# Retention branch's products in sevens, one sum of each block kept in PSUM, and the output weights' low halves on VectorE, in a two-layer gated trunk

## The chip, the cores and the metric

The kernel runs on one core of a Trainium2 chip. The metric is the device time of one execution in microseconds (us); the time of a version is the median of several runs. Engines are named as in the profile: PE (TensorE matmul), PEld (TensorE's weight loads), DVE (VectorE), ACT (ScalarE), POOL (GpSimd), SP (the engine that here only issues DMAs).

## The reference, cut to what matters

Two layers run over 640 tokens (512 noisy ones and 128 of context) with 1024 channels. Each layer makes three branches of 512 channels (retention, latent attention, Fourier mixing). What the change touches is the end of a layer, where each branch is projected to 1024 channels, weighed by a sigmoid gate that is itself a product of the layer's input `h`, summed, and projected once more:

```
branches = jnp.stack([o_r * jax.nn.silu(rz), o_m * jax.nn.silu(mz), o_f * jax.nn.silu(fz)], axis=2)
proj = jnp.einsum('btnw,nwd->btnd', branches, w_branch)
merged = jnp.sum(proj * jax.nn.sigmoid(gl.reshape(B, T, N_BRANCH, D_MODEL)), axis=2)
x = x + gate * (merged @ w_out)
```

All is float32. The kernel gets that precision from a faster matmul type by splitting each operand into a high and a low half and adding three products (high by high, high by low, low by high).

## The kernel before

**The merge stage.** For each of two layers the stage goes through three branches, in the loop over `n`: attention (`n` = 0), retention (`n` = 1), Fourier (`n` = 2). For each branch it goes over four blocks of 256 output channels (the loop over `i`). A block has two parts. The gates' part multiplies `h` (1024 channels) by a piece of `w_in` and ends in a tanh; the products' part multiplies the branch (512 channels) by a piece of `w_branch`, and its result is combined with the gates and added to `mg`, the merged sum. Tokens go in two halves of 320, output channels in two halves of 128.

**Sevens.** `seven` computes a 2 by 2 block product with seven products in place of eight (Winograd's form of Strassen's scheme: sums of the operands are made first, by `hidden_sums`, `branch_sums` and `wsums`). Each product adds into a PSUM bank of 320 columns. Three banks serve one call: A collects products 0, 1, 3 and 5 and is read after each of them, B holds product 2, C products 4 and 6. ACT copies A to SBUF after products 0, 1 and 3, and DVE adds B or C to such a copy. Products 5 and 6 are left to `rest`, which the next call of `seven` pours out by `flush` after its own product 0. A product of the gates' part has 12 matmuls, one of the products' part 6.

**Four.** For the retention branch alone (`n` = 1) the products' part is done by `four`: plain products, 4 accumulations of 12 matmuls, with weights split by `br_plain` and the branch split by `branch_split`. DVE then multiplies each accumulation by the gate straight from PSUM (L1086) and adds to `mg` (L1092).

**PSUM.** There are 8 banks. In this stage `bank` has 6 buffers, and `fill` and `po` take one each (small products for the next modulation vectors run between the others, L187 and L196).

**The output projection.** After the last block, `merge` (L81 on ACT, L82 on DVE) splits `mg` into high and low halves, one row of 128 channels after the other. The weights `w_out` come in 8 tiles of 128x1024: SP loads a tile into one of two `raw` buffers, ACT casts the high half, and the low half is a subtraction (`low`, L74) by DVE for the first tile and by POOL for the other seven. A `raw` buffer is free again when the low half has been made.

**Order.** The order of instructions on each engine is not the order of the code: a scheduler places each where its inputs are ready by its own estimate. Each engine then works through its list in order, and an instruction that waits holds up those behind it.

Of the kernel before, what the change touches and what calls it, by code (L numbers as in the profile page):

```python
# [8 lines left out]
F32 = mybir.dt.float32  # L9
# [5 lines left out]
P = 128  # L15
# [15 lines left out]
def build(nc, tc, A, O):  # L31
# [26 lines left out]
    def bank():  # L58
        return psum["p"].tile([P, 512], F32, name="bank", tag="bank", bufs=6)[:, :320]
# [47 lines left out]
    def rows(w, k0, nk, c0, n):  # L107
        return w[k0 * P:(k0 + nk) * P, c0:c0 + n].rearrange("(k p) n -> p k n", p=P)
# [953 lines left out]
    def br_plain(l, idx, c0):  # L1062
        r = wraw(rows(A["w_branch"][l, idx], 0, 4, c0, 256), 4, 256)
        w = wtiles(4, 256)
        split(w[0], w[1], r, leng=DVE)
        return w

    def branch_split(gp, src):
        for w in range(4):
            hi, lo = (gp.tile([P, 2, 320], F32R, name=f"bq{2 * w + i}", tag=f"bq{2 * w + i}", bufs=1) for i in range(2))  # L1070
            split(hi, lo, h2(src[:, w, :]))
            yield hi, lo

    def four(ws, xs, y2, ms, ps, tick, mid=None, fin=None):
        for j in range(2):
            for h, hs in enumerate(HALF):
                A = bank()
                for k in range(4):
                    for i, (u, v) in enumerate(PASSES):
                        PE.matmul(A, ws[u][:, k, j * P:(j + 1) * P], xs[k][v][:, h, :], start=(k == 0 and i == 0),  # L1080
                                  stop=(k == 3 and i == 2))
                if not (j or h):
                    flush()
                    if mid:
                        mid()
                DVE.scalar_tensor_tensor(ps[j][:, hs], y2[j][:, hs], 1.0, A, op0=ALU.add, op1=ALU.mult)  # L1086
                tick(3 * h)
                if fin:
                    DVE.tensor_tensor(ms[j][:, hs], ms[j][:, hs], ps[j][:, hs], op=ALU.add)
                    fin(j, hs)  # L1090
            if not fin:
                DVE.tensor_tensor(ms[j], ms[j], ps[j], op=ALU.add)  # L1092

# [6 lines left out]
    def seven(ws, xs, y1, y2, last, done, tick):  # L1100
# [16 lines left out]
        ACT.copy(y1[:, a], A)  # L1117
        tick(0)
        flush()
        B = bank()  # L1120
        product(B, 2, True)
        add(y1[:, a], y1[:, a], B)
# [64 lines left out]
    for l in range(DEPTH):  # L1187
# [26 lines left out]
        with ExitStack() as s:  # L1214
# [3 lines left out]
            fillp(), pout()  # L1218
            blocks = [(0, b) for b in range(8, 12)] + [(1, b) for b in range(8)] if l == 0 else [(1, b) for b in range(8, 12)]
# [12 lines left out]
            seven(w0, hq, *zs, lambda ps: ACT.copy(zs[0][:, b], ps), fourier_done, lambda i: None)  # L1232
# [6 lines left out]
            def gates(y2, n, bq, parts, np_):  # L1239
                def last(ps):  # L1240
                    ACT.activation(y2[0][:, b], ps, AF.Tanh, scale=0.5)

                def fin(j):
                    y = y2[j][:, a] if j == 0 else y2[j]
                    ACT.activation(y, y, AF.Tanh, scale=0.5)
# [8 lines left out]
                return last, fin, tick  # L1254

            def products(y2, n, ms, ps):
# [3 lines left out]
                def fin(j):  # L1260
                    y, m, p = y2[j], ms[j], ps[j]
                    s_ = a if j == 0 else slice(0, TT)
                    DVE.scalar_tensor_tensor(p[:, s_], y[:, s_], 1.0, p[:, s_], op0=ALU.add, op1=ALU.mult)
                    if n:
                        DVE.tensor_tensor(m, m, p, op=ALU.add)
                def tick(i):
                    if i in (3, 6):
                        next(steps, None)

                return last, fin, tick  # L1270

            for n, (idx, src, tmp) in enumerate(((1, omt, None), (0, ort, om), (2, ort, om))):
                if n:
                    flush()
                parts = branch_split(gp, src) if n == 1 else branch_sums(gp, src, bql)
                np_ = 4 if n == 1 else 7
# [183 lines left out]
```

## Time and profile before

| | |
|---|---|
| median of 3 runs | 1473.63 us (1472.76 to 1474.07) |
| the profiled execution's own time | 1475.04 us |
| its span, first to last instruction | 1473.3 us |
| PE busy | 1411.6 us, 96% of the span |
| DVE busy | 1025.5 us, 70% |
| ACT busy | 756.2 us, 51% |
| POOL busy | 239.1 us, 16% |
| merge stage, layer 1 / layer 2 | about 428 to 701 us / 1149 to 1401 us |

Busy time is the time in which at least one instruction of the engine ran. Matmuls overlap in their records, so a matmul's own duration (0.31 us for 320 columns) is longer than the distance to the next one, and the distance is what it costs. An engine that is not busy all the time still can hold others up, because of its order.

### The profile page before, as it was taken

What the parts mean: (1) busy time and instruction counts of PE and PEld (TensorE: products, weight loads), DVE (VectorE), ACT (ScalarE), POOL (GpSimd) and SP (SyncE); (2) the same over time, 40 slices, a digit from 0 to 9 for tenths busy, and PEclk for the clock granted to TensorE, in tenths of its full rate; (3) what the DMA queues carried; (4) which work ended last, traced back from release to release, by engine and by line L of the source; (5) the groups of instructions that cost most, each with busy time, mean ns of one, the idle gap of its engine ahead of it and who ended that gap; (6) DMA issues with size and microseconds to landing.
All of it is one profiled execution on the core that took longest, in us unless ns stands there. A gap on an engine that the chain in (4) does not pass through costs nothing.

```text
span 1473.3 us, 25184 instructions
## 1 busy us (share of the span) xinstructions
PE 1411.6 (96%) x9793; PEld 1345.2 (91%) x9793; DVE 1025.5 (70%) x1896; ACT 756.2 (51%) x1607; POOL 239.1 (16%) x227
## 2 busy tenths in 40 slices
PE   6999999999999999999999999999999999999997
PEld 4989989988988989999999899899889899999997
DVE  5367776666887686698573777765759778779843
ACT  5546666544545453455354566664545445445542
POOL 1220000301102211122312100021110112112240
PEclk9999999999999999999999999999999999999999
DMA  9520003331325474233532100042222433323342
GB/s 317 179 76 1 15 16 98 102 84 33 94 90 176 130 221 129 57 85 92 166 101 84 33 15 16 15 138 77 73 73 65 146 108 104 94 80 86 90 125 87
DMA packets 175847, 138.91 MB, mean 94 GB/s; under 512 B 8304, under 2 KB 168688, under 8 KB 175728
## 3 DMA queue, kind: packets, MB, share of 16 engines
q1 hardware_dynamic: 157680, 120.16, 28.1%
q10 hardware_dynamic: 18048, 17.15, 3.7%
q8 instruction: 77, 1.26, 0.4%
q14 instruction: 42, 0.34, 0.1%
HBM read 125.98 MB, written 11.30 MB: 93 GB/s over the span
## 4 chain that ended last, share of the span: by engine, by line
PE 74%; DVE 12%; DMA 5%; ACT 4%; issue 4%; POOL 1%; SPq 0%; POOLq 0%; ACTq 0%; DVEq 0%
PE bank L1109 25%; PE sm L85 6%; PE sm L87 5%; PE sm L86 5%; PE big L269 4%; PE bank L1080 4%; PE big L513 4%; PE fill L319 3%; PE sm L319 3%; PE sm L534 2%; PE sm L526 2%; DVE wl L74 2%; PE fill L187 2%; DMA raw<-in_w_in 1%; PE big L411 1%
## 5 line engine op out<-in xcount | busy, mean ns | idle before, releaser
L74 DVE TENSOR_TENSOR wl<-raw,wh 128x1024 fp32r<-128x1024 f32 (+5 forms) x146 | 153.8, 1055 | 87.3 <-ACT wh L78 39.0
L78 ACT CAST wh<-raw 128x1024 fp32r<-128x1024 f32 (+5 forms) x126 | 104.7, 833 | 86.2 <-DMA raw<-in_w_in 27.9
L1109 PE MATMUL bank<-hh,wh 128*128 128x320 f32 x416 | 130.0, 315 | 5.5 <-ACT tg L1125 4.4
L85 PE MATMUL sm<-wh,hh 128*128 128x256 f32 (+2 forms) x456 | 134.2, 295 | 0.5 <-DVE vl L74 0.5
L86 PE MATMUL sm<-wl,hh 128*128 128x256 f32 (+2 forms) x456 | 133.8, 294 | 0.0
L87 PE MATMUL sm<-wh,hl 128*128 128x256 f32 (+2 forms) x456 | 132.6, 294 | 0.0
L1109 PE MATMUL bank<-hl,wh 128*128 128x320 f32 x416 | 128.6, 310 | 0.0
L1109 PE MATMUL bank<-hh,wl 128*128 128x320 f32 x416 | 127.1, 311 | 0.0
L74 POOL TENSOR_TENSOR wl<-raw,wh 128x1024 fp32r<-128x1024 f32 (+1 forms) x32 | 66.4, 2075 | 294.9 <-ACT wh L78 215.7
L74 POOL TENSOR_TENSOR wl<-st,wh 128x512 fp32r<-128x512 f32 x26 | 38.0, 1463 | 328.8 <-ACT wh L78 328.8
L85 PEld LDWEIGHTS sm<-wh,hh 128*128 128x128 f32 x456 | 87.8, 193 | 2.2 <-issue 0.8
L1109 PEld LDWEIGHTS bank<-hh,wh 128*128 128x128 f32 x416 | 78.3, 188 | 11.9 <-ACT tg L1125 5.2
L86 PEld LDWEIGHTS sm<-wl,hh 128*128 128x128 f32 x456 | 87.8, 193 | 0.1
L87 PEld LDWEIGHTS sm<-wh,hl 128*128 128x128 f32 x456 | 87.4, 192 | 0.4 <-issue 0.4
L1109 PEld LDWEIGHTS bank<-hl,wh 128*128 128x128 f32 x416 | 78.5, 189 | 0.0
L1109 PEld LDWEIGHTS bank<-hh,wl 128*128 128x128 f32 x416 | 78.0, 189 | 0.0
L74 DVE TENSOR_TENSOR ptl<-sm,pth 128x384 fp32r<-128x384 f32 x128 | 67.2, 549 | 13.9 <-ACT pth L78 12.9
L1109 PE MATMUL bank<-bq,wh 128*128 128x320 f32 x320 | 72.0, 311 | 0.0
L78 ACT CAST pth<-sm 128x384 fp32r<-128x384 f32 x128 | 57.2, 481 | 22.6 <-PE sm L526 21.8
L78 ACT CAST wh<-st 128x512 fp32r<-128x512 f32 x68 | 39.6, 618 | 55.1 <-PE bank L1109 53.7
L640 DVE TENSOR_REDUCE nm<-big 128x1 f32<-128x768 f32 x64 | 60.7, 948 | 1.7 <-PE big L513 1.6
L74 DVE TENSOR_TENSOR wl<-st,wh 128x512 fp32r<-128x512 f32 x42 | 40.8, 972 | 29.5 <-ACT wh L78 27.0
(578 smaller groups left out, 4540.3 us busy)
## 6 DMA issues: line engine op xcount, KB each, us to landing
raw<-in_w_in SPq DMA_DIRECT2D x96, 512.0 KB, 4.0
mraw<-in_w_mod ACTq DMA_DIRECT2D x32, 512.0 KB, 4.0
raw<-in_w_branch SPq DMA_DIRECT2D x24, 512.0 KB, 3.6
mraw<-in_w_mod SPq DMA_DIRECT2D x16, 512.0 KB, 9.2
raw<-in_w_out SPq DMA_DIRECT2D x16, 512.0 KB, 4.3
raw<-in_w_in SPq DMA_DIRECT2D x8, 384.0 KB, 6.1
om<-xd SPq DMA_DIRECT2D x16, 192.0 KB, 3.5
xd<-xt SPq DMA_DIRECT2D x8, 320.0 KB, 4.2
```

The source lines that it names most:

```text
L74: eng.tensor_tensor(lo, src, hi.bitcast(F32), op=ALU.subtract)
L78: ACT.copy(hi, src)
L85: PE.matmul(out, ah, bh, start=first, stop=False)
L86: PE.matmul(out, ah, bl, start=False, stop=False)
L87: return PE.matmul(out, al, bh, start=False, stop=last)
L187: PE.matmul(ps[c:c + 32, :n], cs[:, 2 * (j + i):2 * (j + i) + 32], rv[:, i, :], start=(j + i < 4), stop=(j + i >= 4), tile_position=(0, c))
L269: PE.matmul(ps[:, 512 * h:512 * h + 320], ws[a][:, k, :], xs[b][k][:, 320 * h:320 * h + 320], start=(first and k == 0 and i == 0), stop=(l ...
L319: PE.matmul(ps, w[a][:, k, :], (hh, hl)[b][k][:, hs], start=(k == 0 and i == 0), stop=(k == NK - 1 and i == 2))
L513: PE.matmul(S[:, 512 * h:512 * h + 384], qT[hd][a][:, t * P:(t + 1) * P], (kth, ktl)[b][hd % 3][:, 384 * h:384 * h + 384], start=(i == 0), ...
L640: DVE.tensor_reduce(nm, Sv, axis=AX.XY if len(Sv.shape) == 3 else AX.X, op=ALU.max, negate=True)
L1080: PE.matmul(A, ws[u][:, k, j * P:(j + 1) * P], xs[k][v][:, h, :], start=(k == 0 and i == 0), stop=(k == 3 and i == 2))
L1109: PE.matmul(ps, w[u], x[v], start=(first and k == 0 and j == 0), stop=(k == n - 1 and j == 2), skip_group_check=True)
```

## The change

Three edits. First, the retention branch's products go through `seven` too; `four`, `br_plain` and `branch_split` are gone. Second, product 2 no longer has a bank of its own that DVE adds to a copy in SBUF: ACT copies A, after product 0, into a PSUM buffer of a new kind, `pair`, product 2 adds into that, and a new callback `begin` takes the sum from there (a tanh, a copy, or the multiplication by the gate). The first two pair buffers of a stage get one matmul beforehand (`marked`). `bank` falls from 6 buffers to 4, `pair` has 2. Third, the low halves of all eight `w_out` tiles are made by DVE.

```
-        return psum["p"].tile([P, 512], F32, name="bank", tag="bank", bufs=6)[:, :320]
+        return psum["p"].tile([P, 512], F32, name="bank", tag="bank", bufs=4)[:, :320]
+
+    marked = []
+
+    def pair():
+        return psum["p"].tile([P, 512], F32, name="pair", tag="pair", bufs=2)[:, :320]
...
-    def seven(ws, xs, y1, y2, last, done, tick):
+    def seven(ws, xs, y2, begin, last, done, tick):
...
         A = bank()
         product(A, 0, True)
-        ACT.copy(y1[:, a], A)
+        B = pair()
+        if len(marked) < 2:
+            marked.append(PE.matmul(B, ws[0][0][:, 0, :], xs[0][0][0], start=True, stop=True))
+        ACT.copy(B, A)
         tick(0)
         flush()
-        B = bank()
-        product(B, 2, True)
-        add(y1[:, a], y1[:, a], B)
+        product(B, 2, False)
+        begin(B)
         tick(1)
...
+                def begin(ps):
+                    ACT.activation(y2[0][:, a], ps, AF.Tanh, scale=0.5)
+
                 def fin(j):
-                    y = y2[j][:, a] if j == 0 else y2[j]
-                    ACT.activation(y, y, AF.Tanh, scale=0.5)
+                    if j:
+                        ACT.activation(y2[j], y2[j], AF.Tanh, scale=0.5)
...
                 def fin(j):
                     y, m, p = y2[j], ms[j], ps[j]
-                    s_ = a if j == 0 else slice(0, TT)
-                    DVE.scalar_tensor_tensor(p[:, s_], y[:, s_], 1.0, p[:, s_], op0=ALU.add, op1=ALU.mult)
+                    if j:
+                        DVE.scalar_tensor_tensor(p, y, 1.0, p, op0=ALU.add, op1=ALU.mult)
                     if n:
                         DVE.tensor_tensor(m, m, p, op=ALU.add)
+
+                def begin(acc):
+                    DVE.scalar_tensor_tensor(ps[0][:, a], y2[0][:, a], 1.0, acc, op0=ALU.add, op1=ALU.mult)
...
-                parts = branch_split(gp, src) if n == 1 else branch_sums(gp, src, bql)
-                np_ = 4 if n == 1 else 7
+                parts = branch_sums(gp, src, bql)
+                np_ = 7
...
-                    if n == 1:
-                        ends = (lambda: merge(4, 6), lambda j, hs: merge(6 + j, 7 + j, hs)) if (n, i) == (2, 3) else ()
-                        four(br_plain(l, idx, 256 * i), bq, y2, ms, ps, lambda i: next(steps, None) if i else None, *ends)
-                    else:
-                        seven(br_weights(wgp, l, idx, 256 * i), bq, *ps, *products(y2, n, ms, ps))
+                    seven(br_weights(wgp, l, idx, 256 * i), bq, ps[1], *products(y2, n, ms, ps))
...
-                eng = DVE if d == 0 else POOL
                 if d < 4:
-                    ws.append(wload(view, NK, P, eng))
+                    ws.append(wload(view, NK, P, DVE))
                 else:
                     rv = wraw(view, NK, P)
                     w = tuple(xp.tile([P, NK, P], F32R, name=n, tag=n, bufs=4) for n in ("xwh", "xwl"))
-                    split(*w, rv, leng=eng)
+                    split(*w, rv, leng=DVE)
```

How the order moves is shown at two places. The first is PE's list in layer 1, at the start of the gates' part of the retention branch's last block. Before (A is `bank_6905`, B `bank_6919`, C `bank_6946`):

```order
L1109 MATMUL bank_6905<-hh3_152,wl_6882 128x320
L1109 MATMUL bank_6919<-hh4_153,wh_6881 128x320
...
L1109 MATMUL bank_6919<-hh7_156,wl_6882 128x320
L1109 MATMUL bank_6946<-hq1h_4355,wh_6901 128x320
...
L1109 MATMUL bank_6946<-hq1h_4355,wl_6902 128x320
```

After (A is `bank_6921`, the pair buffer `pair_6934`; `bank_6826` belongs to the block before):

```order
L1082 MATMUL bank_6921<-hh3_152,wl_6898 128x320
L1082 MATMUL bank_6826<-bq8_6217,wh_6811 128x320
...
L1082 MATMUL bank_6826<-bq8_6217,wl_6812 128x320
L1082 MATMUL pair_6934<-hh4_153,wh_6897 128x320
L1082 MATMUL pair_6934<-hl4_161,wh_6897 128x320
...
L1082 MATMUL pair_6934<-hh7_156,wl_6898 128x320
```

Before, product 2 stood right behind product 0, into a bank that nothing else had touched; now six matmuls of the block before stand between them, and product 2 needs ACT's copy of A.

The second place is DVE's list at the end of layer 1's merge stage, from the last reads of the banks to the split of the last two rows. Before:

```order
L1113 TENSOR_TENSOR tg_7675<-bank_7763,tg_7675 128x320
L1258 SCALAR_TENSOR_TENSOR om_165<-tg_7674,bank_7817 128x320
L1265 TENSOR_TENSOR mg6_5129<-mg6_5129,om_165 128x640
L1113 TENSOR_TENSOR om_165<-bank_7868,om_165 128x320
L1263 SCALAR_TENSOR_TENSOR om_165<-tg_7675,om_165 128x640
L82 SCALAR_TENSOR_TENSOR hl6_163<-mg6_5129,hh6_155 128x640
L1265 TENSOR_TENSOR mg7_5130<-mg7_5130,om_165 128x640
L82 SCALAR_TENSOR_TENSOR hl7_164<-mg7_5130,hh7_156 128x640
```

After (`wl_7970` and `wl_7976` are the low halves of the third and fourth `w_out` tile):

```order
L1086 TENSOR_TENSOR tg_7712<-bank_7799,tg_7712 128x320
L79 TENSOR_TENSOR wl_7970<-raw_7967,wh_7969 128x1024
L1237 SCALAR_TENSOR_TENSOR om_165<-tg_7711,bank_7853 128x320
L1086 TENSOR_TENSOR om_165<-bank_7903,om_165 128x320
L1244 TENSOR_TENSOR mg6_5129<-mg6_5129,om_165 128x640
L1242 SCALAR_TENSOR_TENSOR om_165<-tg_7712,om_165 128x640
L79 TENSOR_TENSOR wl_7976<-raw_7973,wh_7975 128x1024
L1244 TENSOR_TENSOR mg7_5130<-mg7_5130,om_165 128x640
L87 SCALAR_TENSOR_TENSOR hl6_163<-mg6_5129,hh6_155 128x640
L87 SCALAR_TENSOR_TENSOR hl7_164<-mg7_5130,hh7_156 128x640
```

Two subtractions of 1024 columns, POOL's before, now stand in DVE's list among the steps that lead to `hl6` and `hl7`.

## Rows read from the trace of the kernel before

**Rows 1.** The page: PE's busy time, and the chain that ended last, by engine.
```profile
PE 1411.6 (96%) x9793; PEld 1345.2 (91%) x9793; DVE 1025.5 (70%) x1896; ACT 756.2 (51%) x1607; POOL 239.1 (16%) x227
...
PE 74%; DVE 12%; DMA 5%; ACT 4%; issue 4%; POOL 1%; SPq 0%; POOLq 0%; ACTq 0%; DVEq 0%
```
**Rows 2.** Stretches, layer 1's merge stage: length, busy us of PE, PEld, DVE, ACT, POOL.
```profile
465.00:545.00 80.00, 80.00 (x582) 72.98 (x582) 59.76 (x95) 40.15 (x77) 16.13 (x11) 1.00 0.57 168
545.00:625.00 80.00, 80.00 (x562) 75.80 (x562) 53.28 (x78) 32.23 (x55) 11.02 (x8) 1.00 0.34 95
625.00:690.00 65.00, 65.00 (x445) 65.00 (x444) 58.67 (x93) 34.02 (x66) 15.95 (x11) 1.00 0.32 89
```
**Rows 3.** PE's timeline in layer 1's retention branch: start, duration.
```profile
545.34 0.30 PE L1109 MATMUL bank<-hh,wh 128*128 128x320 f32 x1
...
547.10 0.46 PE L1080 MATMUL bank<-bq,wh 128*128 128x320 f32 x2
```
**Rows 4.** What wrote the banks from `four`: count, ns min/median/max.
```profile
L1080 PE MATMUL bank<-bq,wh x256: 305/309/413, 544.8 to 1322.8; 128*128 128x320 f32 x128
...
L1080 PE MATMUL bank<-bq,wl x128: 307/309/415, 545.2 to 1323.0; 128*128 128x320 f32 x128
```
**Rows 5.** DVE's adds of a bank to a copy (L1113), and their waits.
```profile
L1113 DVE TENSOR_TENSOR tg<-bank,tg x54: 472/481/492, 438.0 to 1399.8; 128x320 f32<-128x320 f32 x54
...
  PE bank L1109: 8.8, 12
```
**Rows 6.** Timeline: product 0's last matmul, and ACT's copy of its bank.
```profile
1389.85 0.31 PE L1109 MATMUL bank<-bq,wl 128*128 128x320 f32 x1
...
1390.20 0.43 ACT L1117 COPY om<-bank 128x320 f32<-128x320 f32 x1 [1.04 <-PE bank L1109]
```
**Rows 7.** Timeline: a copy that came late, and the matmul behind it.
```profile
688.54 0.31 PE L1109 MATMUL bank<-hh,wl 128*128 128x320 f32 x1
...
689.47 1.04 ACT L78 CAST wh<-raw 128x1024 fp32r<-128x1024 f32 x1
...
690.41 0.41 ACT L1131 COPY tg<-bank 128x320 f32<-128x320 f32 x1
...
690.87 0.41 PE L1109 MATMUL bank<-hh,wh 128*128 128x320 f32 x1 [0.56 <-ACT tg L1131]
```
**Rows 8.** DVE's timeline at the end of layer 2's merge stage.
```profile
1400.69 0.49 DVE L1258 SCALAR_TENSOR_TENSOR om<-tg,bank 128x320 f32<-128x320 f32 x1 [0.39 <-PE bank L1109]
1401.22 2.94 DVE L1265 TENSOR_TENSOR mg<-mg,om 128x640 f32<-128x640 f32 x1
...
1405.40 0.82 DVE L82 SCALAR_TENSOR_TENSOR hl<-mg,hh 128x640 fp32r<-128x640 f32 x1
1406.14 0.82 DVE L1265 TENSOR_TENSOR mg<-mg,om 128x640 f32<-128x640 f32 x1
1407.76 2.14 DVE L82 SCALAR_TENSOR_TENSOR hl<-mg,hh 128x640 fp32r<-128x640 f32 x1 [0.81 <-ACT hh L81]
```
**Rows 9.** POOL's timeline there.
```profile
1401.08 2.40 POOL L74 TENSOR_TENSOR wl<-raw,wh 128x1024 fp32r<-128x1024 f32 x1 [0.18 <-ACT wh L78]
1406.38 2.84 POOL L74 TENSOR_TENSOR wl<-raw,wh 128x1024 fp32r<-128x1024 f32 x1 [2.91 <-ACT wh L78]
```
**Rows 10.** TensorE's weight loads there.
```profile
1408.76 0.19 PEld L87 LDWEIGHTS sm<-hh,wl 128*128 128x128 f32 x1
1409.95 0.19 PEld L86 LDWEIGHTS sm<-hl,wh 128*128 128x128 f32 x1 [1.01 <-DVE hl L82]
```
**Rows 11.** DVE's group of 1024-column subtractions, 545 to 625 us: count, busy us, mean ns.
```profile
L74 DVE TENSOR_TENSOR wl<-raw,wh 128x1024 fp32r<-128x1024 f32 x10 | 12.2, 1220 | 8.4 <-ACT wh L1043 7.8 <-ACT wh L78 0.5
```
**Rows 12.** DVE's groups by shape, 625 to 690 us.
```profile
L1022 DVE TENSOR_TENSOR st<-raw 128x256 f32<-128x256 f32 x3 | 4.3, 1419 | 0.1
...
L74 DVE TENSOR_TENSOR wl<-raw,wh 128x512 fp32r<-128x512 f32 x4 | 2.7, 678 | 0.0
...
L1025 DVE TENSOR_TENSOR raw<-raw,st 128x256 f32<-128x256 f32 x4 | 1.6, 412 | 0.0
```

More of the change, by code (lines that the diff above doesn't have):

```diff
@@ L1060, in br_weights @@
         return g(w1, 0), g(w1, 3), g(w1, 1), g(w1, 2), g(w2, 0), g(w2, 1), g(w2, 2)
[L1062 to L1092, printed above, removed]
     tail = []
@@ L1218, in build @@
             fillp(), pout()
+            marked.clear()
             blocks = [(0, b) for b in range(8, 12)] + [(1, b) for b in range(8)] if l == 0 else [(1, b) for b in range(8, 12)]
@@ L1230, in fourier_done @@
                 nc.sync.dma_start(ofd[:, j + 2, :], o)
-            seven(w0, hq, *zs, lambda ps: ACT.copy(zs[0][:, b], ps), fourier_done, lambda i: None)
+            seven(w0, hq, zs[1], lambda ps: ACT.copy(zs[0][:, a], ps), lambda ps: ACT.copy(zs[0][:, b], ps), fourier_done, lambda i: None)
             bql = rp2.tile([P, 4, TT], F32R, name="bql", tag="of", bufs=1)
@@ L1252, in tick @@
                             bq.append(next(parts))
-                return last, fin, tick
+                return begin, last, fin, tick
             def products(y2, n, ms, ps):
@@ L1268, in tick @@
                         next(steps, None)
-                return last, fin, tick
+                return begin, last, fin, tick
             for n, (idx, src, tmp) in enumerate(((1, omt, None), (0, ort, om), (2, ort, om))):
@@ L1282, in build @@
                         y2 = [fl.tile([P, TT], F32, name="tg", tag="th", bufs=2) for _ in range(2)]
-                    seven(gl_weights(wgp, l, C_GL + D * idx + 256 * i), hq, *y2, *gates(y2, n, bq, parts, np_))
+                    seven(gl_weights(wgp, l, C_GL + D * idx + 256 * i), hq, y2[1], *gates(y2, n, bq, parts, np_))
                     if n == 2 and i == 3:
```

## The prediction

> **What bounds the kernel now.** I read the page first: PE is busy 96% of the span and makes up 74% of the chain that ended last [rows 1]. So I asked of each edit whether it takes work from PE or a wait from PE; work taken from another engine counts only where PE waits for that engine. Next the stretches of the merge stage in layer 1, which the change touches: from 465 to 690 us PE is busy without a gap, through all three branches, while DVE goes from 75% busy to 67% in the retention branch and to 90% in the Fourier branch [rows 2]. The reader is to see two things there. PE sets the time of this stage, and 90% of DVE has not yet cost PE anything. The retention branch is the one with DVE to spare, since `four` needs fewer sums. Last I went to the end of the stage, where PE does wait.
>
> **PE's work.** From the start at 545.34 to the one at 547.10 us lie 12 matmuls of 320 columns, so one costs 1.76 / 12 = 0.147 us [rows 3]; its record of 0.31 us overlaps the next. `four` issued 256 + 128 = 384 of them [rows 4]: 2 layers by 4 blocks by 48. A products' part in sevens has 7 by 6 = 42, so 336. The marks add 2 a layer, 4. Net 44 fewer, 44 x 0.147 = 6.5 us. These lie in stretches where PE never waits, so each is on the path, and the whole 6.5 us comes back if PE still never waits. The small modulation products between them keep their number.
>
> **The end of the merge stage.** In layer 2, DVE takes 2.94 us for an addition to `mg` that costs 0.82 elsewhere, and 2.14 for a split that costs 0.82 [rows 8]. Both overlap POOL's subtractions of `w_out` tiles, of 2.40 and 2.84 us [rows 9]. PE runs out of other work and waits for the last `hl`: a weight load starts at 1409.95 where the one before started at 1408.76 [rows 10]. That is 1.19 us against a usual step of some 0.18, 1.0 us at the loads, of which I count 0.85, since a load runs ahead of its matmul. Layer 1 shows the same picture at 705 us. With POOL gone from this stretch, DVE's two slow instructions fall to 0.82 each, 3.4 us less, but the two subtractions of 1024 columns that now stand in that list cost 1.22 each [rows 11]. Net 1.0 us earlier if both tiles have landed. So PE's wait just goes: 2 x 0.85 = 1.7 us. Bounds: nothing lost or gained but the 1.7, up to a loss of 2.4 (both subtractions wait for their tile as well, and what is queued behind them on DVE, the last reads of the banks and `hl6`, `hl7`, is what PE waits for). I take the gain, since a tile's buffer is free 1.2 us sooner than with POOL's 2.4.
>
> **DVE's work.** One add of a bank to a copy goes from each `seven`: 21 calls a layer, 42 x 0.48 [rows 5] = 20 us of DVE in all. The other way, the retention branch now needs weight sums and three more splits per block: one subtraction of 256 columns (0.41, as the sum of that size), two of 512 (0.68), four sums of 256 (0.41, one of them seen at 1.42) [rows 12], for one of 1024 (1.22) [rows 11]. That is 0.4 + 1.4 + 2.7 - 1.2 = 3.3 us, and the block's own sums are 0.8 more than in `four` and 0.5 less by the missing add: some 3.6 us a block. The stretch from 545 to 625 holds a little over four blocks: 53.3 + 15 = 68 us of DVE in 80 - 3.2 = 76.8, 89%. The stretch before it gains the branch's sums and splits (about 6 us) and loses some 4 us of adds, and stays near 77%. So DVE comes to the share that it has in the Fourier branch, 90%, where PE lost nothing [rows 2]. I cost this at nothing; the cover is PE's 0.147 us a matmul, and if it fails the price is in the second rival.
>
> **The new wait.** Product 2 now waits for ACT's copy of A, and PE is in order, so behind it wait 12 (or 6) matmuls of the pair, then product 1. What has to hide the copy is what stands between. In the new list I counted this for all 50 calls: for 40 of them 1.17 us or more of matmuls lie between the end of product 0 and the first matmul into the pair, for 7 it is 0.73 to 0.88, for 3 only 0.29. A copy into PSUM from PSUM is not in the trace; the nearest row is the copy from a bank to SBUF. There the last matmul of product 0 starts at 1389.85, its slot ends at 1390.00, and the copy ends at 1390.63: 0.63 us [rows 6]. At worst a cast of 1024 columns stands ahead in ACT's list: product over at 688.69, copy over at 690.82, 2.1 us [rows 7]. Then the three at 0.29 lose 0.34 to 1.8 each, the seven at 0.8 nothing to 1.3, and the 40 nothing to 0.9. Prompt copies: 1.0 us in all; each late: some 50. I take 0.34 each for the three, 0.3 for the seven, and nothing for the rest, 3.1 us: ACT is about half busy here [rows 2], so half of the times a cast of 1.04 is found under way or ahead, which costs 0.5 to 1, and the margin of 0.1 to 0.25 takes some of it off. That is far nearer to the prompt end than to the late one, since PE has no gap in these stretches with the same kinds of copy. The Trainium skill, "ScalarE: Activation LUTs", section "Step-by-step: what each stage is for", says that a write to PSUM is quicker for ScalarE than one to SBUF, but of use only where TensorE does not need most of PSUM; here all eight banks are taken, so its caveat speaks against this place for the sum. By its first half the 0.63 would be a little shorter and the 3.1 nearer to 2; no run has shown either yet.
>
> **Fewer banks.** With 4 buffers in place of 6, a new A or C waits for the reader of an older one. In the old list the shortest distance from an old bank's last matmul to its next use is 2.05 us of PE's work, and nearly all others 3.8 or more. In the new one three are at 1.9 to 2.4, and 18 at 2.6. The reader takes 0.48 us itself, but only 12 of 126 adds found DVE waiting for PE [rows 5]; the others came when DVE got to them. Bounds: nothing, to 21 x 0.5 = 10 us. I take 1, near the low end, since DVE loses 42 of these very adds.
>
> **The sum.** -6.5 - 1.7 + 3.1 + 1.0 = -4.1 us, and I take 0.2 off for the DVE adds that go in the start of the stage, where PE waits for ACT behind DVE: -4.3. The profiled execution took 1475.04 us, a span of 1473.3 and 1.7 around it, so 1470.7 by that; it was 1.4 above the median of the runs shown, so as a median 1473.63 - 4.3 = 1469.3 us.
>
> **Rivals.** *All waits hidden* (0.18): the copies are prompt and the banks suffice, as nothing made PE wait before in these stretches [rows 2]. Then -6.5 - 1.7 and a little from DVE's relief: 1465.0. Against it speak the three places at 0.29.
>
> *DVE becomes the bound in the retention branch* (0.24). For it: 89% busy, in order, with POOL's weight splits of that branch now slowing it as in [rows 8]. If one more instruction a block is slowed by 1 us (as 1.42 for 0.41 in [rows 12]), 68 us become 72; with the tenth of slack that DVE had in the Fourier stretch [rows 2] that asks for 80 us, 3.2 a layer over PE's 76.8, 6.4 in all. The 4.1 of waits above would lie partly in it, so between 2.0 less and 2.1 more than before: about 1473.7, no change. Against it: PE had no gap in the Fourier stretch with as much DVE work.
>
> *Slower* (0.12): PE waits at every pair. The mechanism is ACT's list: the copy stands behind casts that wait for a weight buffer which PE itself frees late, so that product 2 comes 0.3 us late in each of the 50 calls, 15 us against 8.2 of gain, 1480. It decides from 8.2 / 50 = 0.16 us a call on. For it: the late copy in [rows 7], the one place where ACT had a cast in front. Against it: 40 of 50 places have 1.17 us or more. The Trainium skill, "Perfetto Trace Analysis", section "Optimization Strategy", says that the same gap again and again on the engine that should be full can mean too little PSUM for the next tile; that is how this rival would look, and the trace of before shows no such row.
>
> **How the numbers follow.** The forecast case, 1466.5 to 1470.7, has 0.46; with the three rivals that is all. A difference under 0.2%, 2.9 us, can't be told from no change here. Faster by more: 0.46 + 0.18 = 0.64; within: 0.24; slower: 0.12. The range starts below the case without waits, at 1464.5 (the 0.3 us or so that DVE's relief may bring on top), and goes to 1475.5, past the second rival and the first 2 us of the third; some 0.15 lies outside.
>
> **What would show it.** Right: about 3196 matmuls of 320 columns in place of 3240; the retention stretch some 3 us shorter in each layer with PE still busy throughout; additions to `mg` at the end of the stage at 0.8 us and no wait for `hl` before the output projection's seventh row. The waits of PE then name ACT's copy into the pair, a few times, under 1 us each. Wrong: PE's waits for ACT or for DVE's `wl` in the tens of us; DVE over 95% in the retention stretch; or PE waiting longer at the end of the stage because a tile's subtraction stands ahead of `hl6`.

## The result, and the profile after

The change makes the kernel slower: 1485.8 us (median of 4, 1484.6 to 1488.6) against 1473.2 (median of 4), ratio 1.0096 with a 95% interval of 1.0079 to 1.0113. The forecast was 1469.3 us. The profiled execution of after took 1485.86 us, span 1484.1.

The page of after, its first part (as [rows 1]):

```profile
PE 1414.8 (95%) x9749; PEld 1341.3 (90%) x9749; DVE 1051.8 (71%) x1938; ACT 779.3 (53%) x1663; POOL 233.6 (16%) x221
```

PE has 44 matmuls fewer than before, and its busy time is longer by 3 us. (Busy time also grows when matmuls queue behind a wait, so the count is the surer sign.) The next view is the one to read: stretches of the merge stage of after (us; busy time and count of PE, PEld, DVE, ACT, POOL; granted clock; DMA).

```profile
545.00:625.00 80.00, 78.50 (x532) 75.91 (x531) 70.72 (x104) 43.05 (x81) 17.15 (x12) 1.00 0.35 102
...
597.00:621.50 24.50, 24.50 (x169) 24.50 (x168) 22.98 (x34) 14.00 (x26) 7.13 (x5) 1.00 0.23 66
621.50:640.00 18.50, 17.26 (x113) 16.22 (x112) 18.46 (x28) 11.12 (x20) 4.87 (x3) 1.00 0.32 85
640.00:663.00 23.00, 21.37 (x143) 20.69 (x142) 18.76 (x29) 10.70 (x22) 9.16 (x5) 1.00 0.26 69
...
1253.30:1274.00 20.70, 18.90 (x128) 18.38 (x126) 19.50 (x30) 11.66 (x21) 8.16 (x4) 1.00 0.47 140
1274.00:1296.30 22.30, 20.28 (x126) 20.02 (x126) 15.77 (x25) 11.23 (x21) 3.90 (x3) 0.92 0.29 73
...
1309.00:1333.40 24.40, 24.40 (x168) 24.40 (x167) 22.88 (x33) 14.00 (x26) 7.14 (x5) 1.00 0.23 65
1333.40:1352.00 18.60, 17.37 (x114) 16.32 (x113) 18.57 (x28) 11.12 (x20) 4.97 (x3) 1.00 0.33 86
```

Over the 80 us from 545 to 625, nearly all of them layer 1's retention branch, DVE is busy for 70.72 us, 88%. The Fourier branch begins at 621.5 and 1333.4 us. In its first 18.5 us DVE is busy without a break (18.46 of 18.50, 18.57 of 18.60), and PE, which had no gap before [rows 2], stands still for 1.2 us there and for another 1.6 in the 23 us behind. The last third of the retention branch ahead of it (597 to 621.5 and 1309 to 1333) has DVE at 94% and PE full. The retention branch of layer 2 begins at 1253.3: again DVE at 94% and PE with gaps. The same passage into the Fourier branch in the trace of before:

```profile
1326.60:1345.00 18.40, 18.40 (x128) 18.40 (x127) 17.46 (x28) 10.60 (x21) 6.14 (x3) 1.00 0.30 86
```

DVE was at 95% there already, and PE was full. The room was 5%.

Whom PE waits for in after (us in total, times, longest):

```profile
...
PE pair L1082 <- ACT pair L1093: 4.7, 6, 2.1
...
PE bank L1082 <- ACT tg L1100: 3.4, 2, 1.8
PE bank L1082 <- ACT wh L1048: 3.2, 4, 0.9
PE bank L1082 <- DVE wl L79: 3.1, 6, 0.7
PE bank L1082 <- DVE om L1086: 2.9, 4, 0.9
```

The releasers are of every kind, so this view alone misleads: of the waits in the merge stage it names the pair's copy first. The longest of these waits, followed back through the timeline of after (start, duration, engine, line; in brackets idle time of the engine before it and what ended it):

```profile
1267.88 4.18 POOL L79 TENSOR_TENSOR wl<-st,wh 128x512 fp32r<-128x512 f32 x1 [10.10 <-ACT wh L83]
1268.27 0.82 DVE L79 TENSOR_TENSOR bql<-or,bql 128x640 fp32r<-128x640 f32 x1
1269.01 0.68 DVE L1029 TENSOR_TENSOR raw<-raw,raw 128x512 f32<-128x512 f32 x1
1269.61 0.68 DVE L1030 TENSOR_TENSOR raw<-raw,st 128x512 f32<-128x512 f32 x1
1270.21 0.69 DVE L79 TENSOR_TENSOR wl<-st,wh 128x512 fp32r<-128x512 f32 x1
...
1272.09 1.49 DVE L1027 TENSOR_TENSOR st<-raw 128x256 f32<-128x256 f32 x1 [1.20 <-POOL wl L79]
...
1273.51 0.48 DVE L1086 TENSOR_TENSOR om<-bank,om 128x320 f32<-128x320 f32 x1
1274.02 0.74 ACT L1224 ACTIVATE om<-om 128x640 f32<-128x640 f32 x1 [3.12 <-DVE om L1086]
1274.66 0.42 ACT L1093 COPY pair<-bank 128x320 f32<-128x320 f32 x1
1275.13 0.42 PE L1082 MATMUL pair<-hh,wh 128*128 128x320 f32 x1 [2.06 <-ACT pair L1093]
```

PE waits for the copy. The copy takes 0.42 us, but stands in ACT's list behind a tanh; ACT idles 3.12 us for that tanh, since DVE has not yet added a bank to its input; DVE comes late to the addition because it has first to make the branch's splits (`bql`) and the weight sums, and one of these sums waits for a buffer (`st`) that POOL still reads, in a subtraction that took 4.18 us for a usual 1.5. The wait is named ACT; behind it stand DVE's list and GpSimd's late subtraction. It is not the only one: of GpSimd's 26 subtractions of this kind (`wl<-st,wh`) five take 3.7 to 4.2 us, all of them within 36 us of a branch's beginning (at 637.5, 656.2, 1267.9, 1349.4 and 1368.1 us), and behind each DVE waits 1.2 us for `st`, 6.0 us in all. DVE's group of these sums, in after and then in before:

```profile
L1027 DVE TENSOR_TENSOR st<-raw 128x256 f32<-128x256 f32 x24 | 30.9, 1287 | 6.3 <-POOL wl L79 6.0
...
L1022 DVE TENSOR_TENSOR st<-raw 128x256 f32<-128x256 f32 x16 | 17.8, 1110 | 0.4
```

The end of the merge stage went as forecast. DVE in after, layer 2 (as [rows 8]):

```profile
1415.11 0.81 DVE L1244 TENSOR_TENSOR mg<-mg,om 128x640 f32<-128x640 f32 x1
...
1418.30 0.82 DVE L1244 TENSOR_TENSOR mg<-mg,om 128x640 f32<-128x640 f32 x1
1419.03 0.82 DVE L87 SCALAR_TENSOR_TENSOR hl<-mg,hh 128x640 fp32r<-128x640 f32 x1
```

### The profile page after: what moved, and what is told of

Its sections match the earlier page's. It is cut to its first block, busy times and chain, and to the rows that moved or that the text cites. A ratio compares the mean times of both kernels' runs of the same rounds, so it can differ in the third digit from the quotient of the medians.

```text
span 1484.1 us, 25238 instructions
## 1 busy us (share of the span) xinstructions
PE 1414.8 (95%) x9749; PEld 1341.3 (90%) x9749; DVE 1051.8 (71%) x1938; ACT 779.3 (53%) x1663; POOL 233.6 (16%) x221
## 5 line engine op out<-in xcount | busy, mean ns | idle before, releaser
L83 ACT CAST wh<-raw 128x512 fp32r<-128x512 f32 (+4 forms) x142 | 109.4, 776 | 130.8 <-PE bank L1082 35.3
L79 POOL TENSOR_TENSOR wl<-raw,wh 128x512 fp32r<-128x512 f32 (+1 forms) x34 | 59.2, 1740 | 322.0 <-ACT wh L83 231.4
L1082 PE MATMUL bank<-hh,wh 128*128 128x320 f32 x312 | 98.0, 314 | 3.8 <-ACT tg L1100 3.4
L1082 PE MATMUL bank<-hh,wl 128*128 128x320 f32 x312 | 96.4, 309 | 0.0
L1082 PE MATMUL bank<-hl,wh 128*128 128x320 f32 x312 | 96.4, 309 | 0.0
L1082 PE MATMUL bank<-bq,wh 128*128 128x320 f32 x384 | 87.3, 311 | 0.0
L1082 PEld LDWEIGHTS bank<-hh,wh 128*128 128x128 f32 x312 | 58.6, 188 | 9.3 <-ACT tg L1100 4.3
L1082 PEld LDWEIGHTS bank<-bq,wh 128*128 128x128 f32 x384 | 64.0, 188 | 1.8 <-ACT tg L1220 0.8
L1027 DVE TENSOR_TENSOR st<-raw 128x512 f32<-128x512 f32 (+1 forms) x50 | 55.7, 1119 | 6.3 <-POOL wl L79 6.0
L1082 PE MATMUL bank<-bq,wl 128*128 128x320 f32 x192 | 59.8, 312 | 0.0
```

Of the source, the lines that this page charges most:

```text
L79: eng.tensor_tensor(lo, src, hi.bitcast(F32), op=ALU.subtract)
L83: ACT.copy(hi, src)
L1027: DVE.tensor_tensor(s1, a21, a22, op=ALU.add)
L1082: PE.matmul(ps, w[u], x[v], start=(first and k == 0 and j == 0), stop=(k == n - 1 and j == 2), skip_group_check=True)
```

## The experiments

All were timed in five rounds beside the kernel before. Ratios to it (in each recorded text, theory A and theory B are the two explanations that this run is to tell apart; they change from one group of runs to the next):

| run | what | ratio (95%) |
|---|---|---|
| e1 | before, `w_out` lows on DVE | 0.9984 (0.9971 to 0.9997) |
| e2 | before, retention in sevens | 1.0071 (1.0051 to 1.0091) |
| e3 | before, sum in `pair`, four banks | 1.0059 (1.0038 to 1.0079) |
| e4 | e1 and e2 together | 1.0072 (1.0050 to 1.0095) |
| e5 | e4, lows of the sums replaced by copies on ACT | 1.0038 (1.0023 to 1.0053) |
| e6 | e4, four of these lows on POOL | 1.0146 (1.0128 to 1.0163) |
| e7 | e4, four banks for six | 1.0187 (1.0170 to 1.0203) |
| e8 | e4, `w_out` casts behind the copies | 1.0039 (1.0024 to 1.0053) |
| e9 | e8, lows of the sums left out | 0.9998 (0.9985 to 1.0011) |
| e10 | change, tanh meant to go behind the copy | 1.0093 (1.0076 to 1.0109) |
| e11 | change, lows of the sums left out | 0.9992 (0.9979 to 1.0005) |
| e12 | change, five banks and one pair | 1.0088 (1.0068 to 1.0109) |
| e13 | change, lows left out in retention only | 1.0040 (1.0028 to 1.0052) |
| e14 | change, lows left out in Fourier only | 1.0043 (1.0031 to 1.0055) |
| e15 | before, lows left out | 1.0008 (0.9997 to 1.0019) |
| e16 | change, retention's weight sums left out | 1.0053 (1.0040 to 1.0066) |
| e17 | change, two gates' parts ahead | 1.0073 (1.0052 to 1.0093) |
| e18 | e8, two gates' parts ahead | 1.0131 (1.0108 to 1.0154) |

To see where each gains or loses, this table gives for stretches of PE's list the time from the start of the first matmul of 320 columns to that of the next stretch, less their number times 0.1466 us; layer 1 / layer 2. What is left is waits, the modulation matmuls (nearly all of them in the first column and in layer 1's second), and, where the granted clock fell, slower matmuls (1.5 us of the change's 6.1; last section). The halves of a branch are two blocks each; "last" is the last 100 matmuls.

| | to attention's end | retention, 1st half | 2nd half | Fourier, 1st half | 2nd half | last |
|---|---|---|---|---|---|---|
| before | 22.0 / 14.8 | 7.6 / 0.0 | 0.6 / 0.0 | 0.2 / 0.0 | 0.0 / 0.0 | 0.8 / 0.8 |
| e1 | 21.6 / 13.1 | 7.6 / 0.0 | 0.6 / 0.0 | 0.2 / 0.0 | 0.0 / 0.0 | 0.8 / 0.8 |
| e15 | 20.8 / 11.8 | 7.6 / 0.0 | 0.6 / 0.0 | 0.4 / 0.4 | 0.0 / 0.0 | 0.8 / 0.8 |
| change | 26.8 / 15.0 | 6.7 / 6.1 | 0.1 / 0.2 | 4.5 / 4.6 | 1.3 / 1.4 | 0.0 / 0.0 |
| e2 | 22.0 / 15.7 | 7.7 / 2.3 | 0.6 / 1.1 | 2.9 / 3.4 | 0.2 / 0.0 | 2.9 / 4.6 |
| e3 | 27.0 / 13.8 | 5.5 / 1.1 | 0.2 / 0.2 | 2.0 / 2.0 | 0.1 / 0.1 | 0.3 / 0.3 |
| e4 | 22.0 / 14.8 | 7.7 / 2.4 | 0.6 / 0.2 | 2.9 / 3.7 | 0.2 / 0.1 | 4.4 / 4.3 |
| e8 | 20.7 / 15.7 | 7.7 / 2.4 | 0.6 / 0.0 | 2.9 / 3.8 | 0.2 / 0.0 | 2.0 / 2.0 |
| e9 | 20.9 / 11.6 | 9.1 / 1.2 | 0.6 / 0.0 | 0.6 / 1.9 | 0.0 / 0.0 | 2.0 / 2.0 |
| e10 | 27.3 / 14.5 | 6.6 / 6.1 | 0.1 / 0.2 | 4.2 / 4.3 | 1.3 / 1.5 | 0.0 / 0.0 |
| e11 | 26.6 / 14.3 | 5.4 / 0.7 | 0.0 / 0.0 | 0.9 / 0.9 | 0.0 / 0.0 | 0.5 / 0.5 |
| e12 | 23.8 / 14.3 | 7.9 / 2.7 | 0.3 / 1.5 | 3.5 / 4.2 | 1.3 / 1.7 | 0.5 / 2.6 |
| e13 | 25.5 / 14.9 | 5.4 / 0.7 | 0.0 / 0.0 | 4.4 / 4.3 | 1.3 / 1.3 | 0.0 / 0.0 |
| e14 | 26.4 / 14.9 | 6.6 / 7.0 | 0.1 / 0.2 | 0.9 / 0.9 | 0.0 / 0.0 | 0.5 / 0.5 |
| e16 | 25.9 / 14.1 | 6.0 / 3.0 | 0.2 / 1.1 | 2.5 / 2.5 | 0.0 / 0.0 | 0.5 / 0.5 |
| e17 | 27.5 / 15.4 | 6.1 / 2.3 | 1.8 / 1.8 | 1.6 / 1.7 | 0.0 / 0.0 | 2.7 / 2.7 |

**Each part alone (e1 to e4).** Theory A: the sum in PSUM with its copy and fewer banks costs the time. Theory B: the retention branch's additional work on DVE does. The edits are those of the change, one part at a time; e4 leaves `seven` and the six banks as before.

e1: 

> The kernel before with one part of the change: all eight low halves of w_out are subtracted on VectorE. Both theories: the tail after the merge stage shortens by what the two traces show between them, 1.0 to 1.5 us, and nothing else moves: ratio 0.9990 (1471.7 us). If the tail's gain came from another part of the change, the ratio is 1.000.

e2: 

> The kernel before with one part of the change: the retention branch in sevens, with the old block of seven (six banks, copy to SBUF and add on VectorE). 48 matmuls of 320 columns fewer are worth 48 x 0.147 = 7.1 us. Theory A (the stage's 20 us of new waits come from the sum in PSUM: the copy into the pair, the chain behind it and four banks for six): these waits are absent, 1466 to 1468 us, ratio 0.995 to 0.997. Theory B (they come from the retention branch's weights and sums, which VectorE, GpSimd and ScalarE now have to make in time): -7.1 + 20 = +13, 1486 us, ratio 1.009. Half and half gives 1476.

e3: 

> The kernel before with one part of the change: the sum of a block of seven in PSUM (pair of two, four banks), the retention branch plain as before with the four banks, w_out as before. Theory A: two thirds of the 20 us, as 34 of 50 blocks have a pair, plus 0.6 us for the four marking matmuls: 1486 to 1489 us, ratio 1.009 to 1.010. Theory B: 1474 us, ratio 1.000.

e4: 

> The change without the sum in PSUM: retention branch in sevens with the old block of seven and six banks, and w_out's low halves on VectorE. Theory A: -7.1 - 1.5, 1465 us, ratio 0.994. Theory B: 1484 to 1485 us, ratio 1.008. The difference to the run with the sevens alone is the part of w_out, 1.0 to 1.5 us, in both.

The part of `w_out` gains 0.16%, 2.4 us, by itself; on top of the sevens it gains nothing that can be told (1.0072 in e4, 1.0071 in e2). The sevens, which take away 7.1 us of matmuls, cost 10.4 net, so some 17 us of waits: theory B. But the sum in PSUM costs 8.7 by itself as well, so A is not dead; 5 of these 8.7 us stand in layer 1 ahead of the retention branch (27.0 against 22.0 in the first column). The parts don't add: 10.4 + 8.7 - 2.4 = 16.7 against the change's 14.1 (0.0096 x 1473). In e4 the waits stand in three places: the beginning of the retention branch of layer 2, the beginning of the Fourier branch in both layers, and the last 100 matmuls.

**What the sevens wait for (e5 to e8).** e5 and e6 change how the branch's own sums get their low halves in `branch_sums` (retention and Fourier, `cheap`), e7 only the number of banks, e8 holds the casts of `w_out` back:

```
e5         if cheap:
               ACT.copy(hi, x)
               ACT.copy(lo, x)
           ...
e6         split(hi, lo, x, leng=POOL if cheap and i in (1, 3, 4, 6) else eng)
e7         ... tag="bank", bufs=4)
e8         if d:
               with tc.issue_after(copied[min(d, 2) - 1].ins):   # ACT's last two copies of A
                   ws.append(wload(view, NK, P, DVE))
           ...
```

e5: 

> The change without the sum in PSUM (ratio 1.0072 before), with one thing left out: the seven low halves of the branch's own sums are not subtracted on VectorE for the retention and the Fourier branch; ScalarE writes a copy there instead, so these low halves hold wrong numbers. It takes 7 x 0.81 us from VectorE at each of the four passages from one branch to the next and gives ScalarE 7 x 0.73. Theory A (the passage asks more of VectorE than fits, and PE waits behind it): PE's waits after the passages, 2.9 and 3.7 us into the Fourier branch and 2.4 into the retention branch of layer 2, go: 1473 to 1475 us, ratio 1.001 to 1.003. Theory B (ScalarE's list, with its casts in front of the copies of A, is what is late): ScalarE is later still, 1485 us or more, ratio over 1.009.

e6: 

> The change without the sum in PSUM, with four of the seven low halves of the branch's own sums on GpSimd in the retention and the Fourier branch, nothing left out. VectorE loses 3.2 us at each passage. Theory A (VectorE's amount of work at the passage): about half of the 9 us of waits go, 1477 us, ratio 1.004. Theory B (GpSimd's subtractions slow VectorE's by as much as they take away, as at the end of the merge stage of the kernel before, where 0.82 became 2.94): no gain or a loss, 1482 to 1487 us, ratio 1.007 to 1.011.

e7: 

> The change without the sum in PSUM, and with four bank buffers for six; two banks lie idle. Prediction's own term for fewer banks: 1 us more than with six, 1483 us, ratio 1.008. Rival: the banks are the whole of the 3.5 us by which the sum in PSUM costs on top of the sevens, or more, since here a block of seven needs three of them for two there: 1486 to 1492 us, ratio 1.010 to 1.014.

e8: 

> The change without the sum in PSUM, with ScalarE's casts of the second to fourth tile of w_out queued behind its copies of the last block's A, not in front of them. The last 100 matmuls of the merge stage take 3.6 us more in each layer there than in the kernel before takes them in without waits; the trace shows a cast that waits for its tile ahead of those copies. If that is the cause: 2 x 2.7 us less, 1477 us, ratio 1.0035. If VectorE's arrears are the cause and the cast only stands there: 1482 us, ratio 1.007.

e5 gained 5 us by the ratio, but not in all the places that theory A named: in its trace 6.5 us stay at the beginning of layer 2's Fourier branch, where ACT now works through 13 casts and copies from 1331.9 to 1339.6 us. It doesn't tell A from B, since it moved work. e6 lost 10.9 us: GpSimd takes 2.1 us for what DVE makes in 0.82,

```profile
L74 POOL TENSOR_TENSOR bq<-or,bq 128x640 fp32r<-128x640 f32 x8 | 16.8, 2106 | 6.4 <-ACT bq L78 6.4
```

and PE waits twice as long at the same passages. e7 lost 16.9 us, far over the 1 us expected and over my rival too: with three banks for each block, four are too few; 13 of the 16.9 us stand in layer 1 ahead of the retention branch (35.1 in the table's first column, 22.0 in e4). e8 was as expected. ACT's list at the end of layer 1's stage, first in e4 (the casts wait for their tile, and the copies that PE waits for stand behind them):

```profile
691.91 1.05 ACT L78 CAST wh<-raw 128x1024 fp32r<-128x1024 f32 x1 [1.37 <-DMA raw<-in_w_out]
692.86 0.43 ACT L1241 ACTIVATE tg<-bank 128x320 f32<-128x320 f32 x1
693.19 0.42 ACT L1125 COPY om<-bank 128x320 f32<-128x320 f32 x1
695.00 1.05 ACT L78 CAST wh<-raw 128x1024 fp32r<-128x1024 f32 x1 [1.40 <-DMA raw<-in_w_out]
695.96 0.42 ACT L1131 COPY om<-bank 128x320 f32<-128x320 f32 x1
```

then in e8:

```profile
690.76 0.43 ACT L1126 COPY om<-bank 128x320 f32<-128x320 f32 x1 [0.44 <-PE bank L1110]
691.17 1.05 ACT L78 CAST wh<-raw 128x1024 fp32r<-128x1024 f32 x1
693.46 0.43 ACT L1132 COPY om<-bank 128x320 f32<-128x320 f32 x1 [1.24 <-PE bank L1110]
694.17 1.05 ACT L78 CAST wh<-raw 128x1024 fp32r<-128x1024 f32 x1 [0.28 <-DMA raw<-in_w_out]
```

In e8 the copies wait for PE, as they should. In the change itself this wait is not there (0.0 in the last column), so e8 tells of e4's loss, not of the change's.

**Work at the passage, list order, banks (e9 to e12).**

```
e9, e11    if cheap:
               ACT.copy(hi, x)
               lo = hi              # no subtraction; the matmuls read hi twice
           ...
e10        with tc.issue_after(copied[0].ins):     # the copy into the pair
               ACT.activation(y2[j], y2[j], AF.Tanh, scale=0.5)
e12        ... tag="bank", bufs=5)  ... tag="pair", bufs=1)  ... if len(marked) < 1:
```

e9: 

> The run with the casts behind the copies (ratio 1.0039 before), and the seven low halves of the branch's own sums left out in the retention and the Fourier branch with nothing in their place: the matmuls read the high half a second time, so as many matmuls run. It repairs the run with the lows left out, whose copies went onto ScalarE's list. Theory A (work of VectorE at the passage): the waits of 2.4 us into the retention branch of layer 2 and of 2.9 and 3.8 us into the Fourier branch go, 1464 us, ratio 0.998. Theory B (the order of the lists, not the amount of work): 1477 us, ratio 1.004.

e10: 

> The changed kernel (ratio 1.0096 before), with the gates' second tanh on ScalarE queued behind the next copy into the pair. In its trace the pair's longest waits (2.23, 1.13, 1.10, 0.45 and 0.45 us) stand behind such a tanh, for which ScalarE idles until VectorE has added a bank. Theory A (the copy is late by its place in ScalarE's list): 4 to 5 us less, 1481 us, ratio 1.006. Theory B (VectorE is in arrears and the wait turns up at the next reader of a bank): 1485 us, ratio 1.009.

e11: 

> The changed kernel, with the seven low halves of the branch's own sums left out in the retention and the Fourier branch; the matmuls read the high half a second time. Theory A (VectorE's arrears at the passage are behind the pair's and the banks' waits as well): 8 to 12 us less than the change, 1474 to 1478 us, ratio 1.002 to 1.004. Theory B (copy into the pair and number of banks cost it by themselves): 1483 us or more, ratio 1.008.

e12: 

> The changed kernel with five bank buffers and one pair in place of four and two, and one marking matmul less in each layer. Theory A (too few banks): 3 to 6 us less, 1480 to 1483 us, ratio 1.005 to 1.0075. Theory B (the copy's place in ScalarE's list and VectorE's arrears): within 1 us of the change, ratio 1.009 to 1.010, or more if the single pair is read late.

e10 does not test the order. In its trace a tanh still stands directly ahead of the copy at all the places where one does in the change, among them the longest wait:

```profile
1274.09 0.74 ACT L1234 ACTIVATE om<-om 128x640 f32<-128x640 f32 x1 [3.12 <-DVE om L1088]
1274.73 0.42 ACT L1095 COPY pair<-bank 128x320 f32<-128x320 f32 x1
```

The edit put the tanh behind the copy of the products' part, and the late copy is that of the gates' part after it. So whether another order of ACT's list would help the change stays open. Banks (e12) gain nothing that can be told from the change, though the waits move: layer 2's retention branch loses 2.7 us for 6.1, and 2.6 stand at the end, where there were none. Leaving out 28 subtractions of 0.82 us, 23 us of DVE's work, takes 0.0104 x 1471 = 15.3 us off the change, more than theory A expected, and 6.0 off e8. (DVE's busy time falls by 10 us only, from 1051.8 to 1041.7: others of its instructions take longer.) In e11 PE has 0.5 us of gaps in the Fourier branch's first 18 us, where the change had 1.2:

```profile
621.50:640.00 18.50, 17.97 (x122) 17.65 (x122) 18.36 (x28) 12.14 (x23) 4.18 (x4) 1.00 0.30 86
```

DVE is busy for 99% of this stretch, hardly less than in the change, and PE loses next to nothing. So the share shows that DVE has no slack here, but not how late it is; it does the same passage with 5.7 us less to do.

**Which passage, and whose work (e13 to e16).** e13 and e14 are e11 for one branch alone; e15 does it in the kernel before; in e16 `br_weights` takes the second half of the weights as it is, with no `wsums`, for the retention branch.

e13: 

> The changed kernel (ratio 1.0096 before), with the seven low halves of the branch's own sums left out in the retention branch alone (high half read twice). Theory A (each passage pays for its own work): the waits into the retention branch go, 5.4 us in layer 2 and 1.3 in layer 1, and those into the Fourier branch stay: 1478 us, ratio 1.005. Theory B (VectorE carries arrears from the retention branch into the Fourier branch's passage): those go in part too, 1473 us, ratio 1.002.

e14: 

> The changed kernel, with the seven low halves left out in the Fourier branch alone, where the kernel before made them as well. Theory A (each passage pays for its own work): the waits into and in the Fourier branch go, 2 x (3.7 + 1.3) us: 1476 us, ratio 1.003. Theory B gives the same here, and the pair of runs adds up to more than the 15 us of both together only if arrears are carried.

e15: 

> The kernel before, with the low halves of the branch left out in the retention branch (four there) and the Fourier branch (seven). Both theories: its trace shows PE without a wait at these passages, 0.2 us or less in the Fourier branch, so nothing is gained: ratio 0.998 to 1.000. A ratio under 0.996 would mean that the passages cost the kernel before as well, and that leaving work out gains anyway.

e16: 

> The changed kernel, with the four weight sums of each block left out in the retention branch's products (the second half of the weights is split as it is, so the products are wrong there): 4 x 0.41 us of VectorE in each block, 13 us in all, spread over the branch. Theory A (amount at the passages alone): only the last block's sums lie in the passage to the Fourier branch and the first block's in the one before, 2 to 4 us less, 1482 us, ratio 1.007. Theory B (arrears carried): 8 to 12 us less, 1475 us, ratio 1.002.

0.0056 and 0.0053 make 0.0109, as much as both together (0.0104), and the table shows each clearing its own passage and leaving the other: theory A. e15 gains nothing, so it isn't that less work always helps: in the kernel before these subtractions were hidden. e16 leaves out 32 sums, expected at 0.41 us each, 13 in all; in the trace of the change they take 22, since the first of each block takes 1.1 to 1.5 us beside GpSimd. It gives 6.3 us, between the two theories: half of the waits at each passage go, and those in the Fourier branch's second half entirely. So part of the arrears is carried from block to block.

The five waits of DVE for GpSimd come and go with the passages' work: none is left in e11, four in e13 (the Fourier branch's), one in e14 (the retention branch's). They are a part of the arrears, but not what decides: in e12 one is left, and the time is that of the change. No run takes them away alone, by a third `st` buffer for instance.

**The same work with more time (e17, e18).**

```
-  g0 p0 g1 p1 g2 p2 g3 p3          g: gates' part, p: products' part of a block
+  g0 g1 p0 p1 g2 p2 g3 p3          retention and Fourier branch
```

e17: 

> The changed kernel (ratio 1.0096 before), nothing left out, with the gates' parts of a branch's first two blocks run one after the other, before the first block's products part, in the retention and the Fourier branch. The branch's sums and splits then have 168 matmuls, 24.6 us, to lie beside, where they had 84, 12.3 us. Theory A (too much VectorE work in too short a time at the passages): nearly all of the 15 us that leaving out the low halves gave comes back, 1471 to 1474 us, ratio 1.000 to 1.002. Theory B (VectorE has too much to do over the whole branch, and only taking work away helps): 1483 us or more, ratio 1.008.

e18: 

> The same order of parts on the version with sevens in all three branches, six banks, no sum in PSUM, w_out's low halves on VectorE and its casts behind the copies (ratio 1.0039 before). Theory A: the 9 us of waits after the passages go, 1464 to 1467 us, ratio 0.995 to 0.997, faster than both kernels. Theory B: 1476 us, ratio 1.004.

Both missed. In e17 the waits at the passages do go (layer 2's retention 6.1 to 2.3, the Fourier branch's 5.9 to 1.6 or 1.7), some 13 us together; but some 10 come back: 1.7 us a layer at the pair of the Fourier branch's first block (counted in the column ahead of it), behind a tanh that ACT awaits 2.63 us from DVE, as in the change,

```profile
622.11 0.74 ACT L1224 ACTIVATE tg<-tg 128x640 f32<-128x640 f32 x1 [2.63 <-DVE tg L1086]
622.76 0.42 ACT L1093 COPY pair<-bank 128x320 f32<-128x320 f32 x1
```

and 2.7 a layer at the end, where the change had none. e18 is slower than e8 for the same kind of reason: waits for weights (1.6 and 1.7 us for ACT's `wh` in the two layers' Fourier branches) and 4.8 and 3.8 us at the end. (In e18 the second block's first copy also overwrites half a row of the first block's product before it is added; it issues as many matmuls.) Of the runs that leave nothing out, e1 alone beats the kernel before, at 1468.8 us.

## Why the prediction was wrong, point by point

- **44 fewer matmuls, -6.5 us:** right in number and in price; that they all come back hung on PE never waiting, which failed.
- **End of the merge stage, -1.7 us:** right; 2.4 measured alone in e1, interval 0.4 to 4.3. The addition to `mg` takes 0.82 again.
- **DVE's work, "I cost this at nothing; the cover is PE's 0.147 us a matmul":** this step failed. The amount came out as worked out, 88% over those 80 us for 89%. But I compared it with 90% in the Fourier branch, where PE had lost nothing, and the work isn't spread evenly. The branch's sums and splits can only be made between the last use of the former branch's operands and the first products of the new one, one gates' part (84 matmuls, 12.3 us). There DVE was at 95% before, with the light retention branch next to it; the change put a seven's weight sums and splits on the other side of each passage, and DVE went to 100% and fell behind. Taking 5.7 us of DVE's work from each of the four passages returns 15.3 us (e11), about half of it at either kind of passage alone (e13, e14), and nothing in the kernel before (e15). My rival "DVE becomes the bound" named the cause and sized it at 6.4 us from an average again.
- **The new wait, +3.1:** right where DVE is not in arrears, too small where it is. By the view of waits PE waits at six of the 50 pairs in the change, 4.7 us together, and at four in e11, 1.5; by starts against 0.147 us it is eight, 6.0 us, and four, 2.2. The copy itself costs what I took from [rows 6]. What I missed is that a copy in ACT's list passes on a lateness of DVE: ACT waits for DVE with the tanh ahead of it. The slower rival had the list right but blamed casts.
- **Fewer banks, +1.0:** not settled. A fifth bank in place of the second pair gives back 1.2 us (e12), less than can be told. The sum in PSUM with four banks costs 8.7 us by itself (e3), as much as between e8 and the change. Between e9 and e11, where DVE is relieved, the times are the same, but there e9 has 1.5 us more at the end of each layer's stage.
- **The sum:** with the passages relieved (e11) the change stands at -1.2 us, against -4.3 forecast. Of the other 3 us the traces show 2 to 3 in layer 1's first two columns together. They are 28.4 to 30.0 in seven traces with six banks (before, e1, e2, e4, e8, e9, e15), and 30.8 to 33.9 in the eight with pairs and four banks (the change, e3, e10, e11, e13, e14, e16, e17). (The other three with six banks, in which ACT or GpSimd has more to do or the parts stand in another order, e5, e6 and e18, have 30.5, 33.3 and 31.1.) Between the seven and the eight the difference is in the steps into, between and out of the modulation matmuls, 28.5 to 30.2 us against 31.6 to 32.9. Whether the copy, the banks or the order that follows from them makes these longer, no run separates.

## What to carry to other kernels

An engine's share must be read over the shortest time in which its work has to be done, not over the stage: here a 20 us piece went from 95 to 100% while the 80 us around it stayed under 90, and taking 5.7 us of work out of each such piece gave back 15 of 1485. Even there the share only warns: e11 stood at 99% and lost next to nothing. A releaser in the list of waits is the last link; follow it back (ACT's copy, its tanh, DVE's add, POOL) before pricing a remedy. And look in the trace of an experiment whether its edit moved what it was to move; e10's did not. Cutting buffers wants a run of its own: four banks for six cost 16.9 us in e7, where 1 was expected.

## What the runs showed of the hardware

**GpSimd and VectorE hold each other up both ways.** In the timeline above GpSimd's subtraction of 512 columns took 4.18 us (1.46 on average in the kernel before) while DVE ran subtractions back to back, and DVE's sum of 256 columns took 1.49 us, for 0.41, while the next GpSimd subtraction ran. Of the 24 such sums in after the three beside which GpSimd did nothing took 0.41 to 0.43 us, the other 21 took 1.12 to 1.52. The Trainium skill, "Trainium Architecture — The Big Picture", section "What this means for kernel authors", says that the two share a port pair under an exclusive lock; the trace agrees, and it adds that the late GpSimd instruction can be the one that DVE then waits for.

**A copy from PSUM to PSUM is no quicker than one to SBUF.** ACT in after:

```profile
L1093 ACT COPY pair<-bank 128x320 f32<-128x320 f32 x50 | 20.9, 418 | 22.8 <-PE bank L1082 21.5 <-PE pair L1092 1.1
L1100 ACT COPY om<-bank 128x320 f32<-128x320 f32 x24 | 10.2, 426 | 10.0 <-PE bank L1082 9.5
L1106 ACT COPY om<-bank 128x320 f32<-128x320 f32 x24 | 10.0, 418 | 0.0
```

The Trainium skill, "ScalarE: Activation LUTs", section "Step-by-step: what each stage is for", says that ScalarE writes PSUM more quickly; for this copy, 418 ns against 418 and 426, the measurement says not.

**After a wait of 2 us TensorE ran at half its clock for over 3 us.** After the wait of 2.06 us that ends at 1275.13 the granted clock is 0.50 in the next stretch, the lower of its two levels (1.2 and 2.4 GHz):

```profile
1274.90:1276.00 1.10, 0.87 (x5) 0.87 (x6) 0.02 (x1) 1.10 (x3) 0.00 (x0) 0.94 0.96 276
1276.00:1279.00 3.00, 3.00 (x13) 3.00 (x13) 1.63 (x2) 1.44 (x5) 0.37 (x1) 0.50 0.38 83
1279.00:1280.50 1.50, 1.50 (x11) 1.50 (x11) 1.39 (x2) 0.42 (x3) 0.93 (x1) 0.91 1.00 286
```

12 matmuls start in these 3.0 us, where 20 go at 0.147 each. From 1275.83 to 1279.25 us 13 steps between starts take 3.42 us, for 1.91 at 0.147, so it cost 1.5 us on top of the wait. In the kernel before, a wait of 2.23 us at the start of layer 2's stage was followed by the same (0.91 over 20 us); in e1 that wait was 1.3 us, and the clock stayed at 1.00.
